# Larger block loads in a log-sum-exp kernel: 4 MB DMAs, four block buffers, and a reordered start

## The chip, the cores and the metric

The kernel runs on one core of a Trainium2 chip. The metric is the device time of one execution in microseconds; medians are given with the lowest and highest run. The profile's **span** goes from the program's first to its last profiled instruction and is some 2 us shorter than that time. Engines: PE is TensorE, DVE is VectorE, ACT is ScalarE, POOL is GpSimd, SP is SyncE, which issues the loads.

## The reference, cut to what matters

```python
# x: (8, 2048, 2048) f32, bias: (8, 256) f32;  B, S, D = x.shape;  H = 8, Dh = 256
x_heads = x.reshape(B, S, H, Dh).transpose(0, 2, 1, 3) + bias[None, :, None, :]
x_tiled = np.repeat(x_heads, 2, axis=2)
mx = x_tiled.max(axis=-1, keepdims=True)
lse = mx.squeeze(-1) + np.log(np.exp(x_tiled - mx).sum(axis=-1))     # (8, 8, 4096)
```

Every row of x has eight heads of 256 numbers. Each head needs log(sum(exp(x + bias))), written twice. 134.2 MB are read, 1 MB is written.

## The kernel before

It works on 64 tiles of 2 MB: 128 partitions, two rows of x (16 KB in one run) to a partition, in nine buffers. A tile's load waits for the last use of the tile nine earlier. The work on a tile is spread over four engines: PE adds the bias to heads 0 to 2 with matmuls, POOL adds it to heads 4 to 7, ACT does all exps, and for head 3 the factor exp(bias) is multiplied in afterwards by DVE, which also sums up. From tile 54 on the stages and from tile 57 on the loads get finer, so that little is left to do when the last bytes land.

```python
K = 2
NBUF = 9
STAGES = [(0, (BULK,)), (54, (MIXED,)), (57, (PROMPT_F1, PROMPT_F1)), ...]
...
    def rows_of(t):
        b, blk = divmod(t, NBLK)
        v = x[b, blk * P * K : (blk + 1) * P * K, :]
        if b < B - 1:
            return v.rearrange("(p k) d -> p k d", k=K)
        return v.rearrange("(k p) d -> p k d", k=K)
...
    def load(t):
        after = last_uses[t - NBUF] if t >= NBUF else []
        for k0, k1, c0, c1 in pieces(t):       # one piece a tile; more from tile 57 on
            loads[t, k0, c0] = on_x(t, nc.sync.dma_start(
                out=xts[t % NBUF][:, k0:k1, c0:c1], in_=rows_of(t)[:, k0:k1, c0:c1]), after)
...
    for i in range(3):                         # bias in three bf16 parts, gathered as three rows
        nc.gpsimd.dma_start(out=b3[i : i + 1, :], in_=bparts[:, i])
```

The softmax here doesn't subtract the row's maximum and nothing guards it: scores larger than these inputs give would overflow.

## Time and profile before

| | before |
|---|---|
| time, median of 4 | 326.83 us (326.50 to 327.03) |
| span of the profiled run | 325.4 us |
| DMA engines full with x loads | 98.9% of the span |
| busiest compute engine | POOL, 89% |
| step from tile to tile | 4.894 us |
| last piece of x landed | 319.78 us |

A row of the timeline is start, duration, engine, line, operation, operands, count, and in brackets how long the engine was idle before and what ended that. The prediction below shows the lines themselves. One limit on reading them: one profile is one execution, and its span moves by some 0.3 us between runs.

### The profile page before, as it was taken

What the parts mean: (1) busy time and instruction counts of PE and PEld (TensorE: products, weight loads), DVE (VectorE), ACT (ScalarE), POOL (GpSimd) and SP (SyncE); (2) the same over time, 40 slices, a digit from 0 to 9 for tenths busy, and PEclk for the clock granted to TensorE, in tenths of its full rate; (3) what the DMA queues carried; (4) which work ended last, traced back from release to release, by engine and by line L of the source; (5) the groups of instructions that cost most, each with busy time, mean ns of one, the idle gap of its engine ahead of it and who ended that gap; (6) DMA issues with size and microseconds to landing.
All of it is one profiled execution on the core that took longest, in us unless ns stands there. A gap on an engine that the chain in (4) does not pass through costs nothing.

```text
span 325.4 us, 2350 instructions
## 1 busy us (share of the span) xinstructions
PE 263.2 (81%) x649; PEld 98.6 (30%) x649; DVE 284.0 (87%) x306; ACT 264.7 (81%) x425; POOL 290.7 (89%) x123
## 2 busy tenths in 40 slices
PE   5398999599888789779779788887877897399984
PEld 2033333233323223223223223323223332044442
DVE  1008999999999999998998899989899799999985
ACT  1139999499969878987887969698788778889995
POOL 7999999899999999999999999999999899958874
PEclk9999999899979987997997979798998989569999
DMA  7999999999999999999999999999999999999995
GB/s 293 428 435 429 427 433 422 425 433 429 427 427 431 425 424 433 425 425 434 426 425 431 431 422 427 429 429 427 431 427 426 429 425 429 415 421 421 424 394 154
DMA packets 11934, 135.42 MB, mean 416 GB/s; under 512 B 1361, under 2 KB 1745, under 8 KB 2961
## 3 DMA queue, kind: packets, MB, share of 16 engines
q1 hardware_dynamic: 11824, 135.27, 98.9%
q8 instruction: 5, 0.08, 0.1%
q14 instruction: 7, 0.06, 0.0%
q0 software_dynamic: 96, 0.00, 0.0%
q10 hardware_dynamic: 2, 0.01, 0.0%
HBM read 134.23 MB, written 1.05 MB: 416 GB/s over the span
## 4 chain that ended last, share of the span: by engine, by line
DMA 48%; DVE 35%; POOL 6%; ACT 6%; PE 3%; issue 1%; SPq 0%; DVEq 0%
DMA xt<-in_x_dram 45%; DVE R L350 29%; ACT xt L331 5%; DVE xt L343 5%; POOL xt L325 4%; DMA b<-bparts 2%; PE pair L275 2%; DVE xt L366 2%; PE one_ps L275 1%; ACT xt L293 1%; DMA brow<-in_bias_dram 1%; POOL brest L173 1%; POOL brest L175 1%; PE pair L216 0%; POOL bparts L172 0%
## 5 line engine op out<-in xcount | busy, mean ns | idle before, releaser
L325 POOL TENSOR_TENSOR xt<-xt,b_rep 128x2048 f32<-128x2048 f32 x57 | 258.8, 4543 | 20.1 <-DMA xt<-in_x_dram 20.1
L350 DVE TENSOR_REDUCE R<-xt 128x14 f32<-128x3584 f32 (+1 forms) x56 | 214.5, 3831 | 1.9
L331 ACT ACTIVATE xt<-xt 128x2560 f32<-128x2560 f32 (+5 forms) x77 | 158.1, 2062 | 13.4 <-POOL xt L325 12.5
L275 PE MATMUL pair<-xt,ident 128*128 128x512 f32 x216 | 115.1, 660 | 0.0
L275 PE MATMUL one_ps<-xt,ident 128*128 128x512 f32 x108 | 66.7, 702 | 23.1 <-DMA xt<-in_x_dram 23.1
L293 ACT ACTIVATE xt<-pair 128x1024 f32<-128x1024 f32 x54 | 56.3, 1042 | 20.7 <-PE pair L275 19.3
L275 PEld LDWEIGHTS pair<-xt,ident 128*128 128x128 f32 x216 | 46.2, 214 | 61.5 <-issue 61.5
L343 DVE TENSOR_TENSOR xt<-xt,w_ps 128x512 f32<-128x512 f32 x54 | 36.8, 681 | 27.8 <-ACT xt L331 27.7
L286 ACT ACTIVATE xt<-one_ps 128x256 f32<-128x256 f32 x108 | 40.6, 391 | 7.9 <-PE one_ps L275 7.9
L216 PE MATMUL one_ps<-b,ones 3*128 3x512 bf16 x54 | 20.7, 383 | 18.4 <-ACT xt L286 12.4
L216 PEld LDWEIGHTS <-ones 3*128 3x128 bf16 x162 | 13.5, 92 | 70.2 <-issue 63.8
L216 PE MATMUL pair<-b,ones 3*128 3x512 bf16 x108 | 32.3, 378 | 0.0
L275 PEld LDWEIGHTS one_ps<-xt,ident 128*128 128x128 f32 x108 | 17.0, 198 | 46.4 <-DMA xt<-in_x_dram 39.6
L251 PE MATMUL pair<-xt,ident 128*128 128x512 f32 (+1 forms) x36 | 21.0, 669 | 7.2 <-DMA xt<-in_x_dram 7.1
L286 ACT ACTIVATION_READ_ACCUMULATOR xt<-one_ps 128x1 f32 x108 | 23.5, 218 | 0.0
L366 DVE CUSTOM_DVE_ANT_0 xt<-xt,w_ps 128x256 f32<-128x256 f32 x61 | 22.4, 419 | 0.0
L390 POOL TENSOR_TENSOR xt<-xt 128x128 f32<-128x128 f32 (+3 forms) x39 | 13.9, 356 | 3.1
L382 POOL TENSOR_TENSOR xt<-xt,w_sb 128x256 f32<-128x256 f32 (+1 forms) x13 | 10.1, 773 | 5.4 <-ACT xt L331 4.8
L266 PE MATMUL tpair<-ident 128*128 128x128 f32 x84 | 13.6, 300 | 0.5 <-ACT res L421 0.5
L306 ACT ACTIVATE xt<-pair 128x256 f32<-128x256 f32 x33 | 12.3, 387 | 0.0
L266 PEld LDWEIGHTS tpair<-ident 128*128 128x128 f32 x84 | 11.1, 200 | 4.1 <-issue 3.0
L366 DVE CUSTOM_DVE_ANT_0 xt<-xt,one_ps 128x256 f32<-128x256 f32 x27 | 10.6, 416 | 0.7 <-ACT xt L331 0.7
(40 smaller groups left out, 68.5 us busy)
## 6 DMA issues: line engine op xcount, KB each, us to landing
xt<-in_x_dram SPq DMA_DIRECT2D x57, 2048.0 KB, 30.8
xt<-in_x_dram SPq DMA_DIRECT2D x12, 1024.0 KB, 24.7
xt<-in_x_dram SPq DMA_DIRECT2D x4, 256.0 KB, 11.4
out_dram<-res SPq DMA_DIRECT2D x1, 896.0 KB, 6.6
xt<-in_x_dram SPq DMA_DIRECT2D x2, 384.0 KB, 16.0
xt<-in_x_dram SPq DMA_DIRECT2D x2, 128.0 KB, 6.3
out_dram<-res_last SPq DMA_DIRECT2D x1, 128.0 KB, 1.7
b<-bparts POOLq DMA_DIRECT2D x3, 1.5 KB, 6.4
```

The costliest lines, as they stand in the source:

```text
L216: nc.tensor.matmul(p, lhsT=ones3, rhs=each_row(b3, h * Dh, Dh, K), start=True, stop=False,)
L251: mm = nc.tensor.matmul(p, lhsT=ident, rhs=xts[t % NBUF][:, ka:kb, c : c + w], start=False, stop=True,)
L266: nc.tensor.matmul(tps[B % 2][:, 0], lhsT=ident, rhs=ident, start=True, stop=True)
L275: mm = nc.tensor.matmul(p, lhsT=ident, rhs=xts[t % NBUF][:, :, h * Dh : (h + 1) * Dh], start=False, stop=True,)
L286: act = nc.scalar.activation(out=xts[t % NBUF][:, k, 0:Dh], in_=got[0][:, k * Dh : (k + 1) * Dh], func=ACT.Exp, accum_out=sums[:, k, 0:1],)
L293: act = nc.scalar.activation(out=xts[t % NBUF][:, :, Dh : m["pe"] * Dh].rearrange("p k (h j) -> p h k j", j=Dh), in_=got[-1].rearrange("p ...
L325: add = nc.gpsimd.tensor_tensor(out=v, in0=v, in1=each_row(b_rep, c - G0, D - c, k1 - k0), op=ALU.add)
L331: return on_x(t, nc.scalar.activation(out=v, in_=v, func=ACT.Exp), [after])
L343: mul = nc.vector.tensor_tensor(out=f, in0=f, in1=each_row(w_ps, m["pe"] * Dh - W0, n, k1 - k0), op=ALU.mult,)
L350: red = nc.vector.tensor_reduce(out=sums[:, k0:k1, h0:H], in_=v.rearrange("p k (h j) -> p k h j", j=Dh), op=ALU.add, axis=mybir.AxisListTy ...
L366: ttr = nc.vector.tensor_tensor_reduce(out=v, in0=v, in1=w, scale=1.0, scalar=0.0, op0=ALU.mult, op1=ALU.add, accum_out=dst,)
L390: done = nc.gpsimd.tensor_tensor(out=v[:, :, 0:n], in0=v[:, :, 0:n], in1=v[:, :, n : 2 * n], op=ALU.add)
```

## The change

Its intent: fewer and longer transfers while nothing hurries, the old fine ones at the start and towards the end.

- Tiles 2 to 41 are loaded two at a time, 4 MB in one DMA, four rows of x (32 KB) to a partition. Four block buffers replace nine tile buffers; a block is reloaded when both of its tiles are done.
- For the first five tiles PE adds the bias parts as three one-row matmuls each, and so does not wait for the DMAs that gather them as three rows; ACT issues those DMAs instead of POOL.
- Factors that only the late stages need are made at tile 32.
- Sums, outputs and transposes follow the four-row layout.

```diff
 K = 2
-NBUF = 9
+KB = 4
+BLOCKS = 42
+NBUF = 8
+NEARLY = 5
...
+            blk, i = divmod(at, TB)
+            v = x[b, blk * P * KB : (blk + 1) * P * KB, :]
+            return v.rearrange("(p k) d -> p k d", k=KB)[:, i * K : (i + n) * K]
...
     def load(t):
+        if TB <= t < BLOCKS:
+            if t % TB == 0:
+                after = [u for i in range(TB) if t >= NBUF for u in last_uses[t + i - NBUF]]
+                ins = on_x(t, nc.sync.dma_start(
+                    out=xbs[t // TB % len(xbs)], in_=rows_of(t, TB)), after)
...
-        nc.gpsimd.dma_start(out=b3[i : i + 1, :], in_=bparts[:, i])
+        nc.scalar.dma_start(out=b3[i : i + 1, :], in_=bparts[:, i])
...
+            parts = [(ones3, b3)]
+            if n_ps[0] <= NEARLY:
+                parts = [(ones3[0:1], bparts[:, i]) for i in range(3)]
...
+        if t == T_FACTORS:
+            other_factors()
```

## The prediction

> **What bounds the kernel now.** I read the page first: busy shares, the slices, the DMA queues.
>
> ```profile
> PE 263.2 (81%) x649; PEld 98.6 (30%) x649; DVE 284.0 (87%) x306; ACT 264.7 (81%) x425; POOL 290.7 (89%) x123
> ...
> DMA  7999999999999999999999999999999999999995
> GB/s 293 428 435 429 427 433 422 425 433 429 427 427 431 425 424 433 425 425 434 426 425 431 431 422 427 429 429 427 431 427 426 429 425 429 415 421 421 424 394 154
> ...
> q1 hardware_dynamic: 11824, 135.27, 98.9%
> ```
>
> No compute engine is over 89% busy, while the x loads (queue q1) fill the 16 DMA engines for 98.9% of the span. Only the first slice (start) and the last one (after the loads) are not full. The chain of waits looks otherwise (48% DMA, 35% DVE), but between 26 and 120 us it merely follows VectorE's backlog from a late start. The question is whether the transfer queue ever ran dry because of that. The POOL rows of the timeline answer it, since each add starts when its 2 MB tile has landed:
>
> ```profile
> 28.24 4.55 POOL L325 TENSOR_TENSOR xt<-xt,b_rep 128x2048 f32<-128x2048 f32 x1 [0.16 <-DMA xt<-in_x_dram]
> 33.14 4.55 POOL L325 TENSOR_TENSOR xt<-xt,b_rep 128x2048 f32<-128x2048 f32 x1 [0.34 <-DMA xt<-in_x_dram]
> 38.03 4.54 POOL L325 TENSOR_TENSOR xt<-xt,b_rep 128x2048 f32<-128x2048 f32 x1 [0.34 <-DMA xt<-in_x_dram]
> 42.92 4.56 POOL L325 TENSOR_TENSOR xt<-xt,b_rep 128x2048 f32<-128x2048 f32 x1 [0.35 <-DMA xt<-in_x_dram]
> 47.82 4.56 POOL L325 TENSOR_TENSOR xt<-xt,b_rep 128x2048 f32<-128x2048 f32 x1 [0.34 <-DMA xt<-in_x_dram]
> 53.04 4.55 POOL L325 TENSOR_TENSOR xt<-xt,b_rep 128x2048 f32<-128x2048 f32 x1 [0.67 <-DMA xt<-in_x_dram]
> 58.44 4.52 POOL L325 TENSOR_TENSOR xt<-xt,b_rep 128x2048 f32<-128x2048 f32 x1 [0.85 <-DMA xt<-in_x_dram]
> ```
>
> A tile every 4.894 us: 2.097 MB / 4.894 us = 428.5 GB/s, the same while VectorE was behind and later. The odd steps of 5.2 and 5.4 us coincide with the instruction queues' packets in the packet records (49.4 and 53.3 us, later 116 and 121, 250 and 256): they share the engines, and cost the whole run about 1.8 us (tile 1 lands at 13.54, tile 56 at 284.49; 55 x 4.894 = 269.2 of those 270.95). The windows by stage separate 2 MB from 1 MB loads:
>
> ```profile
> 180.00:210.00 30.00, 24.99 (x55) 8.82 (x55) 29.08 (x14) 24.49 (x39) 27.90 (x7) 0.89 1.01 428
> ...
> 284.00:310.00 26.00, 24.39 (x87) 11.71 (x88) 25.66 (x120) 24.89 (x50) 19.67 (x36) 0.87 1.01 421
> ```
>
> The last two columns are the DMA share and GB/s: full in both, yet 428 with 16 KB packets (2 MB loads) and 421 with 8 KB packets (1 MB loads). So **the kernel is a stream of 134.2 MB at the engines' own rate**, plus a start and a tail. The tail, by the chain in order of time:
>
> ```profile
> 294.48 20.15 DMA xt<-in_x_dram
> 314.63 0.02 issue
> 314.65 1.71 ACT xt L331
> 316.36 0.02 issue
> 316.38 0.42 DVE xt L366
> ```
>
> From the landing at 314.63 the way to the end is 10.7 us (exp, 16 weighted sums of 0.335 us on VectorE, transpose, Ln, the last store), released by that landing.
>
> **What the Trainium skill says.** (1) "DMA: Bandwidth & Descriptors", section Where 436 GB/s comes from: the fabric's ceiling is 435.2 GB/s. The trace agrees: 428.5 held, 435 the best slice. So at most 1.5% of the stream can be won by any shape of load. (2) Same page, section Why small descriptors are slow: each packet has a small fixed overhead, and each descriptor its metadata. The trace agrees in kind: median packets took 309 ns for 8 KB and 611 ns for 16 KB, so 2 x 309 - 611 = 7 ns is fixed. (3) Same page, section Why a DMA increments its semaphore by 16 and not by 1: one descriptor moves one contiguous run, and a run over 64 KiB has to be cut. The trace agrees as far as 16 KB (7,168 such packets); no run yet shows 32 KB as one. (4) Same page, section Issuing engines are not separate DMA queues: moving an issue to another engine saves only sequencer time. Here the three issues kept POOL until 10.16 us, after its last cast had ended at 8.55.
>
> **The change part by part.**
>
> *Block loads.* Tiles 2 to 41 become 20 loads of 4 MB, with four rows of x, 32 KB in one run, to a partition. Each engine carries 8 partitions. Now two tiles take 16 packets of 611 ns and two 9 ns semaphore packets: 9,794 ns (2 x 4,894 = 9,788 measured). As blocks: a 32 KB packet is estimated from the two measured sizes as 2 x 611 - 7 = 1,215 ns; 8 x 1,215 + 9 = 9,729 ns. That is **59 to 65 ns a block, 1.2 us over 20 blocks**, all on the path. If the run is cut into two 16 KB packets, only the semaphore packet goes: 9 ns x 20 = 0.2 us. I put 65% on one packet: expected gain 0.65 x 1.2 + 0.35 x 0.2 = 0.85 us. Tiles 0, 1 and 42 to 63 keep their packet sizes and gain nothing.
>
> *Four block buffers in place of nine tile buffers.* A load now waits for both tiles of the block eight tiles earlier. Before, a steady load was issued 32.4 us ahead of its landing, so a tile was held 9 x 4.894 - 32.4 = 11.6 us. A block's second tile waits one more POOL step (4.55): 16.2 us held of 4 x 9.73 = 38.9, leaving an issue 22.7 us ahead of landing. The transfer itself needs 9.7 and the queue is filled 13 us ahead: not dry. At the start the 16 MB last until about 42.9 us (tile 7 landed at 42.85); even in the old kernel tile 1 was free at 35.05, and it gets earlier. Cost 0.
>
> *Early one-row bias matmuls.* They remove the wait for the bias rows (TensorE's first bias matmul started at 16.93, the parts were ready at 8.55). Five tiles get 9 in place of 3 bias matmuls, 0.21 us apart when warm: +1.3 us on 3.2 us of TensorE a tile, under the 4.9 us that a tile takes to arrive. Tile 0 gets free some 4 to 8 us earlier; only the stream counts, so worth 0 on the end. It is what lets eight tiles suffice.
>
> *Factors at mid-kernel, DMA issues on ScalarE.* About 1.2 us of exp moves to tile 32, where ScalarE has slack (2.34 + 1.02 + 2 x 0.36 = 4.1 us of work in 4.9). Worth 0.
>
> *Lag at the change back to 2 MB.* Tile 42 lands 4.89 us after block 40-41, but POOL needs 9.1 us for that block: 4.2 us behind. It gains 4.894 - 4.55 = 0.345 a tile, 12.2 tiles, so it is caught up at tile 54, where the stages change. Cost 0 to 0.3 us.
>
> *Output layout.* Each batch's Ln runs on 32 partitions x 1,024 instead of 64 x 512: estimated at 1.02 us (as the 128x1024 exp) instead of 0.58, +0.44. Six fall in slack. The seventh, at 294 us, is where ScalarE is full; but it waits for DMAs for 0.28 us at 312 and 0.13 at 314.6, so 0.41 of 0.44 is absorbed. Cost about 0.05 us, up to 0.2 with the lag. The 0.9 MB store landed at 322.0, before the last one was issued (322.74).
>
> **Sum:** 326.91 - 0.85 - 0 + 0.1 = 326.1; with whole 32 KB packets 325.8, with cut ones 326.8. I predict **326.0 us**.
>
> **Rivals.** *The queue runs dry* (four coarse buffers): for it, the release of whole blocks; against it, 13 us of spare by the working above. A dry block would cost several us each, 3 us in all or more: over 329. *Compute takes the lead*: POOL has 4.55 us of work against 4.86 us a tile, 94%; a block that comes in one piece and catch-up that ends just at tile 54 leave little; if it has not caught up, 1 to 3 us pass into the tail: 327 to 328.5. *More is won than packets account for*: at the ceiling of 435.2 GB/s the 40 tiles would take 4.819 us each, 40 x 0.075 = 3.0 us less: 323.9. For it speaks nothing but the best slices; the packet times speak against it. *Hidden anyway*: the start of compute, about 8 us earlier, could be expected to shorten the kernel by that much; against it, the loads never stopped in those 30 us.
>
> **Range and chances.** The two packet cases span 325.7 to 326.8, the tail's uncertainty adds 0.3, and runs differ by 0.15: 8 in 10 between **325.2 and 327.2 us**. Two per cent faster is 320.4, beyond the ceiling's 323.9, unless start or tail get shorter: 0.01. Two per cent slower is 333.4 and needs the queue to run dry again and again: 0.02. Within 2%: 0.97.
>
> **What would show it.** Packets: 2,560 of 32 KB (20 blocks x 128) if right, median near 1,215 ns; none if cut. GB/s in the block stage: 430.5 to 431 (4.194 MB / 9.73 us) if right, 428.5 to 429 if cut, under 425 if the queue runs dry. The DMA share stays full in all slices but the first and last; block issue to landing about 22 us. VectorE's first reduce well before 26.6 us with the end barely moved. The landing that releases the tail's exp at 313.4 to 314.5, and 10.7 us from there to the end. The prediction is wrong if POOL still waits for nothing at tile 56 (lag not worked off), if a DMA gap shows, or if a block's period is neither 9.73 nor 9.78 us.

## The result

| | before | after |
|---|---|---|
| time, median of 4 | 326.83 us (326.50 to 327.03) | 325.43 us (325.22 to 325.89) |
| span of the profiled run | 325.4 us | 323.1 us |
| last piece of x landed | 319.78 us | 317.59 us |
| from there to the span's end | 5.59 us | 5.56 us |

The ratio is 0.996 (95% interval 0.9943 to 0.9977). Ratios are the mean time of one kernel's runs over that of the other's of the same rounds, so not quite the ratio of the medians. The change is real and small: within 2%, and inside the predicted range.

The page of the kernel after, in the same parts as the prediction showed of before (busy shares, slices, DMA packets and queue):

```profile
PE 270.3 (84%) x691; PEld 102.9 (32%) x691; DVE 283.9 (88%) x306; ACT 265.8 (82%) x426; POOL 287.7 (89%) x120
...
DMA  8999999999999999999999999999999999999995
...
DMA packets 8830, 135.42 MB, mean 419 GB/s; under 512 B 1041, under 2 KB 1425, under 8 KB 2417
...
q1 hardware_dynamic: 8720, 135.27, 98.6%
```

The DMA engines are still full from start to end. (Slices of this kernel's page read up to 457 GB/s, since the whole of a long packet falls into one slice: a single slice says nothing about a ceiling.) What changed is how the bytes are cut: 8,720 packets on the load queue where there were 11,824. The packet records hold 2,560 packets of 32 KB, 128 for each of 20 blocks; their median is 1,215 ns and their commonest duration 1,213, where the commonest of 16 KB, twice, is 2 x 611 = 1,222.

POOL's rows of the timeline show the rhythm:

```profile
23.21 9.03 POOL L376 TENSOR_TENSOR xb<-xb,b_rep 128x2048 f32<-128x2048 f32 x2 [5.32 <-DMA xb<-in_x_dram]
32.92 9.02 POOL L376 TENSOR_TENSOR xb<-xb,b_rep 128x2048 f32<-128x2048 f32 x2 [0.68 <-DMA xb<-in_x_dram]
42.64 9.05 POOL L376 TENSOR_TENSOR xb<-xb,b_rep 128x2048 f32<-128x2048 f32 x2 [0.70 <-DMA xb<-in_x_dram]
```

Two tiles arrive at once, and the step between blocks is 32.92 - 23.21 = 9.71 us (9.715 as the mean of the undisturbed landings), against 2 x 4.894 = 9.788 before: **73 ns a block, 20 x 73 ns = 1.46 us**. The landings agree: tile 1 landed 0.22 us earlier than before, tile 41 (about 208.55 against 210.31) 1.76 us. So 1.54 us came within the blocks.

The lag at the change back to 2 MB, again in POOL's rows:

```profile
208.62 54.09 POOL L376 TENSOR_TENSOR xb<-xb,b_rep 128x2048 f32<-128x2048 f32 x12 [0.67 <-DMA xb<-in_x_dram]
262.92 4.54 POOL L376 TENSOR_TENSOR xb<-xb,b_rep 128x2048 f32<-128x2048 f32 x1 [0.21 <-DMA xb<-in_x_dram]
```

From block 40-41 POOL adds twelve tiles without a pause and then, at tile 52, waits for a DMA again: it has caught up, two tiles before the stages change.

The tail, by the chain in order of time:

```profile
312.54 1.60 ACT xb L382
314.14 0.02 issue
314.16 0.42 DVE xb L417
```

The same exp that before was released by a DMA at 314.65 now starts when ACT is free, 0.2 us after its row had landed (312.34). From that landing to the end it is 10.8 us, as before (10.7). ACT's own rows of the timeline, kernel before first, then after:

```profile
312.09 1.70 ACT L331 ACTIVATE xt<-xt 128x1792 f32<-128x1792 f32 x1 [0.28 <-DMA xt<-in_x_dram]
```

```profile
310.15 1.68 ACT L382 ACTIVATE xb<-xb 128x1792 f32<-128x1792 f32 x1
```

The 0.28 us that ACT used to wait here are gone: work fills them (the batch's Ln now takes 1.01 us).

Not all of the span's gain reached the time. In every run of the changed kernel the time is 2.1 to 2.2 us longer than the span; for the kernel before it is 1.7 to 1.8. Spans fell by 1.6 us (medians 325.0 and 323.4 of nine runs each), the time by 1.1 to 1.4. That 0.4 us lies outside what the profile shows.

### The profile page after: what moved, and what is told of

It is laid out like the page before. It is cut to its first block, busy times and chain, and to the rows that moved or that the text cites. A ratio compares the mean times of both kernels' runs of the same rounds, so it can differ in the third digit from the quotient of the medians.

```text
span 323.1 us, 2398 instructions
## 1 busy us (share of the span) xinstructions
PE 270.3 (84%) x691; PEld 102.9 (32%) x691; DVE 283.9 (88%) x306; ACT 265.8 (82%) x426; POOL 287.7 (89%) x120
## 3 DMA queue, kind: packets, MB, share of 16 engines
q1 hardware_dynamic: 8720, 135.27, 98.6%
## 4 chain that ended last, share of the span: by engine, by line
DMA 40%; POOL 18%; ACT 17%; PE 14%; DVE 9%; issue 0%; SPq 0%; DVEq 0%
DMA xb<-in_x_dram 40%; POOL xb L376 18%; ACT xb L382 11%; DVE R L401 6%; PE pair L326 5%; PE one_ps L326 3%; PE pair L267 3%; ACT xb L357 2%; PE one_ps L267 2%; DVE xb L417 2%; PE pair L219 1%; ACT xb L337 1%; DVE xb L394 1%; ACT res L471 1%; ACT xb L344 1%; DMA brow<-in_bias_dram 1%
## 5 line engine op out<-in xcount | busy, mean ns | idle before, releaser
L376 POOL TENSOR_TENSOR xb<-xb,b_rep 128x2048 f32<-128x2048 f32 x57 | 257.6, 4539 | 20.7 <-DMA xb<-in_x_dram 20.6
L401 DVE TENSOR_REDUCE R<-xb 128x14 f32<-128x3584 f32 (+1 forms) x56 | 214.5, 3830 | 1.9
L382 ACT ACTIVATE xb<-xb 128x2560 f32<-128x2560 f32 (+5 forms) x77 | 157.1, 2050 | 10.3 <-POOL xb L376 10.1
L326 PE MATMUL pair<-xb,ident 128*128 128x512 f32 x216 | 114.3, 656 | 0.0
L326 PE MATMUL one_ps<-xb,ident 128*128 128x512 f32 x108 | 67.5, 710 | 11.5 <-DMA xb<-in_x_dram 11.5
L344 ACT ACTIVATE xb<-pair 128x1024 f32<-128x1024 f32 x54 | 55.5, 1027 | 23.2 <-PE pair L326 23.0
L326 PEld LDWEIGHTS pair<-xb,ident 128*128 128x128 f32 x216 | 46.2, 214 | 61.3 <-issue 61.3
L394 DVE TENSOR_TENSOR xb<-xb,w_ps 128x512 f32<-128x512 f32 x54 | 36.7, 681 | 26.2 <-ACT xb L382 26.2
L337 ACT ACTIVATE xb<-one_ps 128x256 f32<-128x256 f32 x108 | 40.0, 380 | 6.6 <-PE one_ps L326 6.6
L417 DVE CUSTOM_DVE_ANT_0 xb<-xb,w_ps 128x256 f32<-128x256 f32 x61 | 22.4, 418 | 0.0
L417 DVE CUSTOM_DVE_ANT_0 xb<-xb,one_ps 128x256 f32<-128x256 f32 x27 | 10.6, 415 | 0.1
## 6 DMA issues: line engine op xcount, KB each, us to landing
xb<-in_x_dram SPq DMA_DIRECT2D x20, 4096.0 KB, 21.5
xb<-in_x_dram SPq DMA_DIRECT2D x17, 2048.0 KB, 22.7
xb<-in_x_dram SPq DMA_DIRECT2D x12, 1024.0 KB, 22.7
```

Source lines behind the costliest of these rows:

```text
L326: mm = nc.tensor.matmul(p, lhsT=ident, rhs=xts[t % NBUF][:, :, h * Dh : (h + 1) * Dh], start=False, stop=True,)
L337: act = nc.scalar.activation(out=xts[t % NBUF][:, k, 0:Dh], in_=got[0][:, k * Dh : (k + 1) * Dh], func=ACT.Exp, accum_out=sums[:, k, 0:1],)
L344: act = nc.scalar.activation(out=xts[t % NBUF][:, :, Dh : m["pe"] * Dh].rearrange("p k (h j) -> p h k j", j=Dh), in_=got[-1].rearrange("p ...
L376: add = nc.gpsimd.tensor_tensor(out=v, in0=v, in1=each_row(b_rep, c - G0, D - c, k1 - k0), op=ALU.add)
L382: return on_x(t, nc.scalar.activation(out=v, in_=v, func=ACT.Exp), [after])
L394: mul = nc.vector.tensor_tensor(out=f, in0=f, in1=each_row(w_ps, m["pe"] * Dh - W0, n, k1 - k0), op=ALU.mult,)
```

## The experiments

My theory: the load stream is the bound and the gain is in the packets; the other parts are worth nothing by themselves. The rivals: larger or fewer DMAs give the gain whatever their runs; the earlier start of compute gives it; blocks cost something at the changes. Each group of runs shares its runs of the kernel before (medians 326.79, 326.85 and 326.76 us).

### The yardstick

The changed kernel once more, unedited.

> The changed kernel once more, as the yardstick of this group: 325.4 us, 1.3 to 1.5 us under the kernel before.

Measured 325.67 us (325.29 to 325.82), ratio 0.9962 (0.995 to 0.9975). As expected.

### All loads 2 MB again

```diff
-BLOCKS = 42
+BLOCKS = 2
```

> The changed kernel with every load cut back to 2 MB or less; eight tile buffers, early bias and late factors stay. Packet theory: the whole gain goes, 20 blocks x 73 ns (9,788 before, 9,715 measured for a block) = 1.5 us more than the changed kernel, 326.8 to 327.0, with 16 KB packets of 611 ns. Rival (the gain comes from the earlier start of compute or from what else changed): 325.4. Rival (eight buffers are worse than nine): above 327.2.

Measured 326.92 us (326.82 to 327.14), ratio 1.0005 (0.9992 to 1.0017), last piece of x landed at 319.09 us, 1.5 us after the changed kernel's. The whole gain goes with the block loads; the early start, the late factors and eight instead of nine buffers bring nothing measurable.

### 4 MB in one DMA, but in 16 KB runs

The block's two tiles come from two separate stretches of rows.

```diff
-                        out=xbs[t // TB % len(xbs)], in_=rows_of(t, TB)
+                        out=xbs[t // TB % len(xbs)].rearrange("p (h k) d -> p h k d", k=K),
+                        in_=split_rows_of(t),     # x block as "(h p k) d -> p h k d"
```

> The blocks stay 4 MB in one DMA and are released as before, but the two tiles of a block are taken from two separate stretches of rows, so that a partition's run is 16 KB (wrong rows in the outputs, on purpose). Packet theory: 16 x 611 + 9 = 9,785 ns a block, so nearly the whole gain goes: 326.7 to 326.9. Rival (fewer or larger DMAs give the gain, whatever their runs): 325.4.

Measured 327.00 us (326.71 to 327.04), ratio 1.0004 (0.9991 to 1.0018). The DMA view of this run, its packets and its issues:

```profile
DMA packets 11390, 135.42 MB, mean 417 GB/s; under 512 B 1041, under 2 KB 1425, under 8 KB 2417
...
xb<-in_x_dram SPq DMA_DIRECT2D x20, 4096.0 KB, 21.4
```

There are still 20 DMAs of 4 MB, released as in the changed kernel, but 2,560 more packets. Undisturbed blocks landed 9.785 us apart, the number expected. So **between 2 and 4 MB the length of the run counts here, not the size or the number of DMAs**.

### 4 MB in one DMA, in 8 KB runs

The same with four stretches, "(k p) d -> p k d".

> As runs_16k, but with a partition's four rows from four separate stretches: 8 KB runs (wrong rows in the outputs, on purpose). Packet theory: 32 x 309 + 9 = 9,897 ns a block, 182 more than the 9,715 of the changed kernel, x 20 = 3.6 us: 329.0. Rival (only the size of a DMA counts): 325.4.

Measured 330.17 us (329.72 to 330.50), ratio 1.0095 (1.0078 to 1.0112): the direction and the order of size are right, but 1.2 us more than expected, above all in the blocks (20 x 38 ns = 0.8 us). Undisturbed blocks took about 9.935 us, not 9.897. With the three lengths side by side, 32 packets an engine take 9.935 us, 16 take 9.785 and 8 take 9.715: 9.4 and 8.8 ns for each packet saved. The 7 ns of the prediction were too few. They were said to come from median durations; 309 and 611 are the commonest ones in the packet records, and the medians of the kernel before are 313 and 613, so its 7 ns rest on the choice of figure.

### The start as it was

Bias rows from the first tile on, their DMAs issued from POOL, all factors at the start; the blocks stay.

```diff
-NEARLY = 5
+NEARLY = 0
...
-        nc.scalar.dma_start(out=b3[i : i + 1, :], in_=bparts[:, i])
+        nc.gpsimd.dma_start(out=b3[i : i + 1, :], in_=bparts[:, i])
...
+    other_factors()           # here instead of at tile 32
```

> The changed kernel with its start as it was: bias rows of three from the first tile on, their DMAs issued from POOL, all factors made at the start. My theory: the stream of loads does not notice, 325.2 to 325.7, with VectorE's first reduce at about 26.6 us instead of 21.9 and block 8-9 issued at about 35 us instead of 32, still before the queue is empty at 42.6. Rival (the blocks need the early start): a gap in the DMA share near 43 us and 1 us or more on the end.

**A miss.** Measured 326.69 us (326.18 to 327.38), ratio 0.9999: 1.0 us more than the changed kernel, with a wide spread. PE's rows of the timeline show a part that I had not foreseen, the first bias matmul of this run and, in the second fence, of the changed kernel:

```profile
20.64 0.58 PE L269 MATMUL one_ps<-b,ones 3*128 3x512 bf16 x1 [11.92 <-DMA b<-bparts]
```

```profile
8.50 1.48 PE L267 MATMUL one_ps<-bparts,ones 1*128 1x512 bf16 x3
```

The rows landed at 20.6 us, not at 16.8 as in the kernel before (6.6 to 10.5 us from issue, against 5.8 to 7.1). Tile 1 was free at 39.9 us instead of 35, and block 8-9 was issued at 40.0, only 1.8 us before the last packet of the block ahead ended. The DMA share did dip at 38 to 44 us (0.91 where the changed kernel has 0.99), and fifteen packets at 41 us took up to 1.87 us instead of 1.21. But the share was 1.04 in the ten us after, and against the changed kernel's, the landings only went from 0.22 us early at block 6-7 to 0.13 late at block 10-11. Even this third of a microsecond can't be put down to the short lead: from the landing of block 6-7 to that of block 10-11 it is 20.64 us here, and as much in the next run, where the same blocks were issued 7.0 and 7.9 us before the queue's end. A further 0.9 us had been lost by the block that landed at 199.9, with leads of 8 to 12 us where it was lost; instruction packets fell differently there, but that they are the cause is only argued. Part of that came back (0.57 behind at tile 56), and 0.6 us more was lost from there to the end. So a short lead lengthened packets in this trace; **what cost the 1.0 us is not settled**.

### One part of the start at a time

Only the early matmuls undone (NEARLY = 0):

> The changed kernel without the one-row bias matmuls; the three bias rows are still issued from ScalarE and the factors still made late. The old start cost 1.0 us (326.69 against 325.67), and in its trace blocks 8-9 and 10-11 were issued only 1.8 and 2.9 us before the packets of the block ahead of them ended, and took 10.1 and 10.5 us instead of 9.71. Short-lead theory: here the rows land at about 15 us, not 20.6, tile 1 is free at about 34, the lead is 7 us or more, and nothing is lost: 325.3 to 325.9. Rival (the early matmuls themselves carry the 1 us): 326.5 to 326.9.

Measured 325.30 us (325.11 to 325.65), ratio 0.9953 (0.9939 to 0.9967). The first bias matmul started at 15.46 us, block 8-9 was issued 7.0 us before the queue's end. Nothing is lost; it may even be a little faster than the changed kernel, but the intervals overlap.

Only the issue moved back to POOL:

> The changed kernel with the DMAs of the three bias rows issued from POOL as before; early matmuls stay. Short-lead theory: the rows are first needed at tile 5, about 42 us, so they may land at 20 us: 325.3 to 325.9. Rival (the issue from POOL itself costs the 1 us, by disturbing the loads or POOL's first adds): 326.5 or more.

Measured 325.60 us (325.32 to 325.99), ratio 0.9965 (0.9953 to 0.9978). Nothing lost either, although these rows too took up to 10.5 us to land: with the one-row matmuls they are not needed before tile 5.

So each of the two early parts can be undone alone without loss. The microsecond was gone only in the run that undid both and made all factors at the start; the factors were not moved back by themselves, so it isn't shown which of the three, or which pair, it needs.

### Where the blocks end

BLOCKS = 56 and BLOCKS = 48 in place of 42.

> Blocks up to tile 55 instead of 41. Packets alone: 7 more blocks x 73 ns = 0.5 us less, 324.9. Lag theory: tile 54 lands with tile 55, so POOL is 4.2 us behind when the stages change, and ScalarE, which works through the tail without a break, hands on most of it: 3 to 4 us more, 328 to 329.5.

> Blocks up to tile 47. Lag theory: 4.2 us behind at tile 48, 0.345 us worked off a tile, 2.1 us left at tile 54; less 3 x 73 ns: 1 to 2 us more, 326.3 to 327.4. Packets alone: 325.2.

Measured 329.17 us (328.56 to 329.74), ratio 1.0069 (1.0049 to 1.0088), and 326.18 us (326.01 to 326.50), ratio 0.9979 (0.9964 to 0.9994). The last x landed 0.55 and 0.3 us earlier than in the changed kernel, as the packets promise (7 and 3 blocks of 73 ns), and from there to the end it took 10.6 and 6.8 us instead of 5.6 to 5.9. POOL's row of the timeline with 56, and the window of 284 to 310 us (busy time of PE, PEld, DVE, ACT, POOL; clock, DMA share, GB/s) with 56 and, in the last fence, in the changed kernel:

```profile
277.07 13.54 POOL L376 TENSOR_TENSOR xb<-xb,b_rep 128x2048 f32<-128x2048 f32 x3 [0.69 <-DMA xb<-in_x_dram]
```

```profile
284.00:310.00 26.00, 22.19 (x71) 10.93 (x72) 25.87 (x117) 26.00 (x49) 18.93 (x31) 0.75 1.01 419
```

```profile
284.00:310.00 26.00, 25.39 (x97) 12.43 (x97) 25.46 (x129) 25.59 (x53) 19.30 (x38) 0.87 1.01 420
```

Tiles 54 and 55 come together and tile 56 queues behind them, so POOL is done with it at 290.6 instead of 287.1, and ACT, busy in all of the 26 us, has no pause in which to catch up. The lag theory agrees with both runs; for 48 it was too dark by 0.1 us at the nearer end.

### Three block buffers

NBUF = 6, with tile 63 loaded one tile later, and reloads waiting for one more kind of sum in the fine stages, so that no buffer is overwritten while it is read.

> Three block buffers instead of four (tile 63 is loaded one tile later, so that no buffer is overwritten early). My working: a block is held 16.2 us of 29.1, so it is issued 12.9 us ahead, 3 us more than the transfer needs: steady blocks just fit, but at the start the queue is empty at 32.9 us while tile 1 is free at 32.2, with about 1 us from issue to the first packet; gaps of 1 to 2 us in each of the first two or three turns: 327.5 to 331. Rival (buffers have ample slack at three too): 325.4.

**A miss, far beyond the range:** 343.03 us (340.50 to 343.84), ratio 1.048 (1.0438 to 1.0522). The x loads by source line in this run and, in the second fence, in the changed kernel (shortest, median and longest time from issue to landing):

```profile
L158 SPq DMA_DIRECT2D xb<-in_x_dram x20: 327/328/1014, 1.6 to 208.6; - x20
...
DMA to landing us min/median/max: 12.3/14.4/30.0
```

```profile
L158 SPq DMA_DIRECT2D xb<-in_x_dram x20: 327/328/997, 1.6 to 187.3; - x20
...
DMA to landing us min/median/max: 17.9/21.5/34.5
```

A block was issued a median of 14.4 us before it landed; I had worked out 12.9 and held that to be enough for a transfer of 9.7. It is not. By the packet records the later blocks were issued 1.3 to 4.5 us before the block ahead ended, and landed 9.7 to 12.3 us after it; the first two, issued 0.4 us before and 0.8 us after the queue's end, took 11.6 and 13.0. The page says how:

```profile
q1 hardware_dynamic: 8720, 135.27, 95.0%
```

95.0% of 341.7 us is 324.6 us of packet time, against 98.6% of 323.1 = 318.6: the same bytes took 6 us more while they moved, and the engines had nothing for 12.6 us more (17.1 against 4.5). How much lead is enough, the packets show better than the landings, which scatter (leads of 2.8 to 3.0 us: 9.7 to 12.3 us). In the run with the old start the three blocks with leads of 1.8, 2.9 and 4.3 us have 15, 9 and 16 packets of over 1,235 ns among 128, and those with 5.0 us or more at most two, near instruction packets; in the changed kernel, whose shortest lead after the start is 7.1 us, it is at most three. **In these runs packets lengthened in blocks that were issued up to some 4.5 us before the queue ran out, and, those few aside, in none issued 5 us before.** Why they do, no run here shows; nor does every such block land late, as the run with the old start shows.

### The same memory in 2 MB loads

The run before with BLOCKS = 2.

> The same 12 MB of buffers as in the run with three blocks (343.0 us), but loads of 2 MB or less. Short-lead theory: a tile is held 11.6 us of 6 x 4.89, so in the steady state it is issued some 13 us before the queue is empty and nothing is lost; at the start tiles 10 to 12 get leads of 2.5 to 4 us and may lose 0.3 us each: 327 to 329. Rival (12 MB of buffers are too few whatever the load): 335 or more.

Measured 331.31 us (329.90 to 333.01), ratio 1.0141 (1.0109 to 1.0173). Up to tile 56 the theory holds: its add starts at 284.31 us, 0.28 after the run with eight 2 MB buffers (284.03), where three blocks stood at 297.60. So up to there 12 MB suffice for 2 MB loads and not for 4 MB ones. The packets agree with the runs above: tiles 9 to 11, issued 2.4 to 3.6 us before the queue's end, have 53 lengthened packets (over 640 ns), tiles 12 to 15, issued 4.2 to 4.9 us before it, none. But 3.5 us were lost after tile 56, where the fine pieces had fewer buffers and tile 63 its later load; I had not counted that, and which of the two it was is not separated.

### The layout of the outputs

KB = 4 becomes KB = 2: 2 MB loads, and sums and outputs laid out as before.

> The changed kernel with blocks of two rows to a partition, so all loads are 2 MB and the layout of sums and outputs is the kernel before's (64 partitions, 2 KB runs in the store). Against all_2mb (span 324.8, time 326.92) only the layout differs. Expected: the span as there within 0.4. In every run of the changed family the time is 2.1 to 2.2 us longer than the span, in the kernel before 1.75 to 1.8: if that comes from the output's layout the time is 326.5 here, otherwise 326.9.

Measured 327.16 us (327.11 to 327.28), ratio 1.0012 (0.9998 to 1.0026), spans 325.0 to 325.1. The span is as expected, and the time is still 2.1 us longer. So the 0.4 us outside the span does not come from the layout; nor from the block loads (all_2mb: 2.1) or the early parts (old_start: 2.1 to 2.2). Its cause stays open.

## Why the prediction was right or wrong, point by point

- **What bounds the kernel: right.** The DMA engines stay full, and the time moved by what the stream's landings moved.
- **Block loads: right, mis-sized.** The 32 KB run went out as one packet, and its commonest duration was 1,213 ns, against 1,215 foretold from the commonest ones of 8 and 16 KB (called medians there). The term of the sum was 59 to 65 ns a block, held back further by the 65% chance to 0.85 us; measured were 73 ns and 1.46 us in the stream. By the steps of the blocks a packet saved is worth about 9 ns, not 7. The sum itself comes to 326.16 us, and 326.0 was named. Three run lengths with the same DMAs, and 2 MB loads with the same start, show that this is the whole gain.
- **Four buffers: right for four, wrong in its reasoning.** Issue to landing was 21.5 us (22.7 foretold), and the queue stayed full. But the step "the transfer itself needs 9.7 and the queue is filled 13 us ahead: not dry" took any lead above zero to be free. Three buffers showed that up to some 4.5 us it need not be.
- **"Even in the old kernel tile 1 was free at 35.05 ... Cost 0": right for this kernel, where block 8-9 was issued at 32.17 us, 9.8 before the queue's end; its reason failed.** With blocks and the old start the tile was free at 39.9, because the bias rows landed later. That run lost 1.0 us; that the late release is why is not shown.
- **Ceiling: weak support.** "435 the best slice" was no sign of one: the changed kernel's slices read up to 457 GB/s. The steady rate, 4.194 MB in 9.715 us or 431.7 GB/s, stays below the 435.2 of the page.
- **Early matmuls: the cost was wrong, without effect.** I had them under the 4.9 us that a tile takes to arrive. PE's rows of the timeline of the changed kernel:

```profile
17.77 0.82 PE L267 MATMUL one_ps<-bparts,ones 1*128 1x512 bf16 x3
...
24.10 0.95 PE L267 MATMUL one_ps<-bparts,ones 1*128 1x512 bf16 x3
...
35.56 0.82 PE L267 MATMUL one_ps<-bparts,ones 1*128 1x512 bf16 x3
...
42.08 0.38 PE L267 MATMUL one_ps<-b,ones 3*128 3x512 bf16 x1
```

  Tile to tile it was 6.3 us at first and 6.5 for the last (42.08 - 35.56): nine bias matmuls stand between the drained bank and the next x matmuls (the granted clock was 0.72 at 38 to 44 us). DVE started at 21.2 instead of 25.9 us, and by tile 4 the advantage was used up. Without them the kernel is no slower.
- **Lag: right.** Caught up at tile 52 instead of 54; longer blocks brought it into the tail.
- **Tail: right in size, wrong in release.** I expected the landing to release the last exp, at 313.4 to 314.5 us. It came at 312.34, before that range, as the stream gained more than foretold and the profile of before is at the long end. ACT released the exp, 0.2 us later, and the way from landing to end grew by less than 0.1 us.
- **Hidden anyway: right** for the start of compute; **not foreseen**: 0.4 us of the gain lost outside the span.

## What to carry to other kernels

In a kernel whose DMA engines never pause, look at packet durations by size: the fixed part of a packet times the number of packets saved is what larger loads won here, and it took longer contiguous runs, not larger DMAs. Before making loads coarser, work out how long before the queue's end each one is issued, with the start's delays in it, and keep some 5 us beyond zero, the lead from which these runs showed hardly a lengthened packet. Where a coarse stage meets a fine one, count how many steps the engine with the least slack needs to catch up, and change over that much earlier.

## What the Trainium skill lacked or had wrong

- "DMA: Bandwidth & Descriptors", Why small descriptors are slow, gives the fixed cost of a packet as about 3 cycles plus 32 bytes of metadata, and no figure for large ones. Here a packet saved is worth about 9 ns between 8 and 32 KB (blocks of 4 MB: 9.935, 9.785 and 9.715 us).
- The same page, Rules for kernel authors, asks for 1 MiB or more per DMA for bandwidth; it names no length of run. With loads queued ahead, 4 MB and 2 MB DMAs of the same 16 KB runs came out alike (327.00 and 326.92 us); only the run length counted.
- No page says how far ahead a load must be queued: blocks issued 1.3 to 4.5 us before the queue's end landed up to 12.3 us after the one ahead instead of 9.71.
- The same page, Queues, rings and completion order, names row 14 as runtime-internal, without what it costs. Here instruction packets came on q14 and on q8 as well (seven of 8 KB, about 0.31 us each, and five of 16 KB, about 1.07 us), and single landings near them came 5.4 or 5.6 us after the one before instead of 4.89.
- The same page says that issuing from another engine saves only sequencer time. The three issues of 1.5 KB bear it out on the end (325.60 against 325.67 us), but the time from issue to landing differed: 6.6 to 10.5 us from POOL and 5.5 to 6.4 us from ACT, beside the same block loads.
